# Matmul order inside a weight item: the products with the rounded weights first, those with the rest last

## The chip, the cores and the metric

One core of one Trainium2 chip runs the whole layer. The metric is the device time of one execution in microseconds (us); the figure given for a kernel is the median of its runs. PE is the matmul engine (TensorE), PEld its loads of the stationary operand, ACT is ScalarE, DVE is VectorE, POOL is GpSimd, and SP issues the DMAs that bring the weights.

## What is computed

One encoder layer on 256 tokens of width 2048 in float32: a norm, one input projection, eight heads of dilated attention beside eight heads of bidirectional retention, an output projection, and a SwiGLU feed-forward layer of width 5632, with residuals and a last norm. The part that the change touches is the second half:

```
h = h + mixed @ w_out
n2 = rmsnorm(h, norm_ffn_w)
h = h + (silu(n2 @ w_gate) * (n2 @ w_up)) @ w_down
return rmsnorm(h, norm_final_w)
```

## The kernel before

The matmuls run in a rounded form of float32 (float32r). To keep the precision, each operand is split in two: a rounded copy and a rest, which is the value less its rounded copy. A product a·w is then made of three matmuls: rounded with rounded, rounded with the weights' rest, and the activations' rest with the rounded weights. In the code `x[0]`, `x[1]` are the rounded and the rest part of the activations (the stationary operand, 128x128), `w[0]`, `w[1]` those of the weights (the moving operand, 128x512).

From the output projection on, the products are "by tokens": tokens are the rows of the result, and the weights stream past as tiles of 128 x 1024, one DMA of 512 KB each. A `Block` is a result of 256 tokens by 1024 columns (o0, o1 of the output projection, gu0 to gu10 of gate and up, d0_0 to d2_1 of down). It runs a list of items written in `ORDERS`. An item named "C" is a plain product: one weight tile serves four banks of PSUM (2, 3, 4 and 8: two token halves by two column halves), three matmuls each, twelve in all. An item with a number, 1 to 7, is one of the seven products of a Strassen scheme: one weight tile, one bank, six matmuls (two halves of the contraction, three each). "K" and "Z" are plain products of the last block, whose split weights are kept. "H" and "T" stand for the gating of the block before and for the transposes of its result (names `pt_h`, or `pt_n` for the normed input), "M" for the sums that join the seven products.

For each weight tile the work goes through three engines: SP loads the raw tile (`rawc`, `raw`, into a few fixed buffers), ACT copies it into the rounded half of a `ws` tile (L524), DVE subtracts to get the rest into the other half (L527), and PE multiplies (L581). There are five `ws` buffers and the split is issued three items ahead. Every instruction of ACT, DVE, POOL and PE in this part is chained to the one recorded before it on the same engine (`ch`), so each engine works in the order in which the code is written. DVE and ACT have other work in the same queue: DVE ends the blocks (`part`, `ht`), makes the sums of tiles, and the gating product (L758).

`Block.three` (L576 to L582) issues the three matmuls of one product; `classical` picks bank, activations and column half for one quarter of an item; `run` goes through the steps of an item and calls `done`, which lets DVE end a bank after its last matmul.

Of the kernel before, what the change touches and what calls it, by code (L numbers as in the profile page):

```python
# [88 lines left out]
def encoder_layer(ctx: ExitStack, tc: tile.TileContext, xT, x, gains, gain_f, decay, tab, w_qk, w_in, w_st, y):  # L89
# [8 lines left out]
    nc = tc.nc  # L98
# [31 lines left out]
    def wtile(name):  # L130
        return wsp.tile([P, 4, 2, CB], F32R, tag="ws", name=name)
# [134 lines left out]
    for c in range(KT // 2):  # L266
# [6 lines left out]
        src = w_qk[c].rearrange("p (k c) -> p k c", c=CB)  # L273
# [8 lines left out]
        ws = wtile(f"ws_first{c}")  # L282
        for k in range(0, 4, step):
            w, r = ws[:, k:k + step], half[:, k:k + step]
# [218 lines left out]
    def ch_ins(ins):  # L503

        if ins.engine in queue:
            tc.add_manual_dep(
                ins, queue[ins.engine].name,
                mybir.DependencyInfo(mybir.DependencyClass.NoSync, mybir.DependencyReason.DATA), reason="stream",
            )
        queue[ins.engine] = ins  # L510

    def ch(ins):
        ch_ins(ins.ins)
# [43 lines left out]
    class Block:  # L557
# [16 lines left out]
                self.banks[r] = ps1(f"p{r}_{self.name}")  # L574
            return self.banks[r]

        def three(self, r, x, w):

            for u, v in ((0, 0), (0, 1), (1, 0)):
                self.left[r] -= 1  # L580
                ch(nc.tensor.matmul(self.bank(r), x[u], w[v], start=r not in self.begun, stop=self.left[r] == 0))  # L581
                self.begun.add(r)  # L582

        def done(self, *rs):
            for r in rs:
# [50 lines left out]
            return ws  # L636

        def classical(self, ws, k, i, n):
            self.three((2, 3, 4, 8)[2 * i + n], self.quarter(self.a[k // 2], 2 * (k % 2) + i), ws[n])

        def run(self, what, m, ws):
            if what == "M":
                self.mid()
            elif what == "C":
                for i in range(2):
                    for n in range(2):
                        self.classical([[ws[:, q, v] for v in range(2)] for q in range(2)], m, i, n)
                self.done(2, 3, 4, 8)
            elif what == "K":
                self.kept.append((m, [[w[:, v] for v in range(2)] for w in ws]))  # L650
                for n in range(2):
                    self.classical(self.kept[-1][1], m, 0, n)
                self.done(2, 3)
            elif what == "Z":
                for n in range(2):
                    for k, w in self.kept:
                        self.classical(w, k, 1, n)
                    self.done((4, 8)[n])
            elif isinstance(what, int):
                src, q = {1: (self.a, 0), 2: (self.a, 2), 3: (self.sa, 3), 4: (self.a, 3),  # L660
                          5: (self.sa, 0), 6: (self.sa, 1), 7: (self.sa, 2)}[what]
                for u in range(2):
                    self.three(what, self.quarter(src[2 * m + u], q), [ws[:, u, v] for v in range(2)])
                if what in (2, 3, 4):
                    self.done(what)
            elif self.hooks.get(what):
                self.hooks[what].pop(0)()
# [149 lines left out]
    for i, (b, what, m) in enumerate(stream):  # L817
        done += i in work
        for k in work[:done + AHEAD]:
            if k >= i and k not in ready:  # L820
                c, w, n = stream[k]
# [78 lines left out]
```

## Time and profile before

| | us |
|---|---|
| median of 3 runs | 1170.35 (1169.21 to 1172.95) |
| the profiled execution | 1173.2 |
| its span | 1171.0 |
| PE busy | 1139.8 (97%) |
| DVE busy | 971.2 (83%) |
| ACT busy | 673.4 (58%) |
| stretch of the products by tokens (L581) | from 367 to 1161 of the span |

The profile is one execution. The page gives shares of the span; a busy PE in it is a modelled one, since the end of a matmul is not observed. More is learned from the starts: the timeline merges instructions of the same kind that follow each other into a row (start, length, count), and the difference of two rows' starts over the count is what one matmul costs there. A row ends in square brackets where the engine stood idle before it, with the instruction that ended the wait.

### The profile page before, as it was taken

The numbers are of one execution on the slowest core, as the hardware profiler recorded it, in microseconds if no ns is written. First come the engines' busy times: TensorE is split into PE (matmuls) and PEld (weight loads), VectorE is DVE, ScalarE is ACT, GpSimd is POOL, SyncE is SP. The second block draws the span as 40 slices with busy tenths as digits, with TensorE's granted clock in tenths as the row PEclk, the third lists the DMA queues.
The fourth block names the chain that finished last, engine by engine and source line by source line (L and its number), as shares of the span: only waits on it lengthen the run. The fifth ranks groups of instructions, "written<-read, shape, count | busy, mean of one in ns | idle before, by whom it ended". The sixth has DMA issues, their size and how long they took to land.

```text
span 1171.0 us, 15265 instructions
## 1 busy us (share of the span) xinstructions
PE 1139.8 (97%) x5546; PEld 953.4 (81%) x5546; DVE 971.2 (83%) x1053; ACT 673.4 (58%) x824; POOL 202.2 (17%) x198
## 2 busy tenths in 40 slices
PE   7999999999999999999999999999999999999996
PEld 5888888888887877878888878788888877888885
DVE  8887787576677787779998888899989878999985
ACT  6355555555655565556656555566666555666653
POOL 8432232112122110010000021000100202000011
PEclk9999999999999999999999999999999999999998
DMA  8664555555556877659888899988988899889785
GB/s 324 200 232 151 191 190 166 167 178 166 163 171 180 266 215 219 211 174 259 257 249 247 274 262 252 301 228 247 262 265 235 239 319 245 277 255 289 236 215 156
DMA packets 77115, 267.37 MB, mean 228 GB/s; under 512 B 8816, under 2 KB 8816, under 8 KB 77040
## 3 DMA queue, kind: packets, MB, share of 16 engines
q1 hardware_dynamic: 61920, 221.29, 54.3%
q0 software_dynamic: 14400, 44.05, 21.0%
q10 hardware_dynamic: 720, 1.07, 0.2%
q8 instruction: 43, 0.70, 0.2%
q14 instruction: 32, 0.26, 0.1%
HBM read 220.23 MB, written 2.10 MB: 190 GB/s over the span
## 4 chain that ended last, share of the span: by engine, by line
PE 74%; DVE 12%; DMA 7%; issue 4%; ACT 3%; POOL 0%; SPq 0%; DVEq 0%; POOLq 0%; ACTq 0%
PE p_gu L581 29%; PE p_d L581 13%; DVE ws_gu L527 3%; DMA rawc_d<-in_w_st 3%; PE ps_qr L157 3%; PE ps_va L164 3%; PE ps_gr L157 3%; PE ps_vr L164 3%; PE ps_kr L157 3%; PE p_o L581 2%; PE ps_ka L157 2%; DMA rawc_gu<-in_w_st 2%; PE ps_qa L157 2%; DMA rawc_o<-in_w_st 1%; DVE ws_o L527 1%
## 5 line engine op out<-in xcount | busy, mean ns | idle before, releaser
L581 PE MATMUL p_gu<-ws_gu,n 128*128 128x512 f32 x1482 | 355.9, 392 | 6.4 <-DVE ws_gu L527 4.8
L581 PEld LDWEIGHTS p_gu<-ws_gu,n 128*128 128x128 f32 x1482 | 278.4, 188 | 69.1 <-DVE ws_gu L527 8.9
L581 PE MATMUL p_d<-ws_d,h 128*128 128x512 f32 x708 | 168.9, 390 | 2.0 <-DVE ws_d L527 1.8
L527 DVE TENSOR_TENSOR ws_gu<-rawc_gu,ws_gu 128x1024 fp32r<-128x1024 f32 x113 | 137.7, 1220 | 29.2 <-ACT ws_gu L524 28.0
L581 PEld LDWEIGHTS p_d<-ws_d,h 128*128 128x128 f32 x708 | 132.6, 188 | 31.2 <-DVE ws_d L527 2.9
L524 ACT ACTIVATE ws_gu<-rawc_gu 128x1024 fp32r<-128x1024 f32 x113 | 118.8, 1056 | 53.5 <-PE p_gu L581 28.6
L581 PE MATMUL p_gu<-ws_gu,sa_n 128*128 128x512 f32 x504 | 128.5, 391 | 0.0
L581 PEld LDWEIGHTS p_gu<-ws_gu,sa_n 128*128 128x128 f32 x504 | 93.9, 188 | 19.2 <-DVE ws_gu L527 0.2
L527 DVE TENSOR_TENSOR ws_gu<-raw_gu,ws_gu 128x1024 fp32r<-128x1024 f32 x84 | 102.4, 1219 | 1.5 <-ACT ws_gu L524 0.5
L524 ACT ACTIVATE ws_gu<-raw_gu 128x1024 fp32r<-128x1024 f32 x84 | 88.5, 1054 | 22.3 <-PE p_gu L581 18.5
L527 DVE TENSOR_TENSOR ws_d<-rawc_d,ws_d 128x1024 fp32r<-128x1024 f32 x54 | 65.8, 1220 | 20.5 <-ACT ws_d L524 19.8
L524 ACT ACTIVATE ws_d<-rawc_d 128x1024 fp32r<-128x1024 f32 x54 | 57.2, 1059 | 37.8 <-DMA rawc_d<-in_w_st 19.8
L524 ACT ACTIVATE ws_gu<-rawt_gu 128x1024 fp32r<-128x1024 f32 x42 | 44.3, 1056 | 55.7 <-DVE rawt_gu L527 40.4
L537 POOL DMA_DIRECT2D raw_gu<-raw_gu x21 | 18.1, 862 | 290.9 <-DVE rawt_gu L527 209.9
L581 PE MATMUL p_d<-ws_d,sa_h 128*128 128x512 f32 x240 | 61.2, 390 | 0.0
L527 DVE TENSOR_TENSOR ws_gu<-rawt_gu,ws_gu 128x1024 fp32r<-128x1024 f32 x42 | 51.2, 1219 | 5.4 <-ACT ws_gu L524 5.4
L581 PEld LDWEIGHTS p_d<-ws_d,sa_h 128*128 128x128 f32 x240 | 44.8, 188 | 9.2
L524 ACT ACTIVATE ws_d<-raw_d 128x1024 fp32r<-128x1024 f32 x40 | 42.2, 1055 | 12.6 <-PE p_d L581 11.4
L527 DVE TENSOR_TENSOR ws_d<-raw_d,ws_d 128x1024 fp32r<-128x1024 f32 x40 | 48.7, 1219 | 0.7
L157 PE MATMUL ps_gr<-n,ws_gr 128*128 128x512 f32 x128 | 45.6, 399 | 0.0
L164 PE MATMUL ps_va<-ws_va,n 128*128 128x512 f32 x128 | 45.6, 399 | 0.0
L157 PE MATMUL ps_qr<-n,ws_qr 128*128 128x512 f32 x128 | 45.5, 399 | 0.0
(258 smaller groups left out, 2270.4 us busy)
## 6 DMA issues: line engine op xcount, KB each, us to landing
rawc_gu<-in_w_st SPq DMA_DIRECT2D x113, 512.0 KB, 5.2
raw_gu<-in_w_st SPq DMA_DIRECT2D x63, 512.0 KB, 5.3
rawc_d<-in_w_st SPq DMA_DIRECT2D x58, 512.0 KB, 5.1
raw_d<-in_w_st SPq DMA_DIRECT2D x30, 512.0 KB, 5.1
rawc_o<-in_w_st SPq DMA_DIRECT2D x23, 512.0 KB, 5.0
raw_gu<-raw_gu POOLq DMA_DIRECT2D x21, 512.0 KB, 7.4
raw_gu<-rawt_gu POOLq DMA_DIRECT2D x21, 512.0 KB, 5.6
raw_va<-in_w_in SPq DMA_DIRECT2D x16, 512.0 KB, 3.9
```

What stands on the lines that cost most here:

```text
L157: nc.tensor.matmul(ps[:, f, :], t[:, j, 0, f * P:(f + 1) * P], a, start=start, stop=False)
L164: nc.tensor.matmul(ps[:, f, :], a[:, 0, f * P:(f + 1) * P], t[:, j, :, :], start=first, stop=False)
L524: ch(nc.scalar.activation(out, src, func, **kw))
L527: ch(nc.vector.tensor_tensor(out, x, y, op=op))
L537: ch(nc.gpsimd.dma_start(out, other, accum_op=ALU.add))
L581: ch(nc.tensor.matmul(self.bank(r), x[u], w[v], start=r not in self.begun, stop=self.left[r] == 0))
```

## The change

Inside an item the matmuls are put in another order. Before, each bank (or, in a numbered item, each half of the contraction) had its three matmuls in a row: rounded with rounded, rounded with the weights' rest, the activations' rest with rounded. Now all matmuls that read the rounded weights come first, over all banks of the item, and those that read the weights' rest come last. A "C" item so has eight matmuls on the rounded half and then four on the rest; a numbered item four and two; a "K" item four and two. In the last "C" of a block (where `left[2] == 3`) and in "Z" the banks still follow each other, with the rest last inside each bank. The number of matmuls, weight loads and all other instructions is the same.

```
-        def three(self, r, x, w):
-
-            for u, v in ((0, 0), (0, 1), (1, 0)):
-                self.left[r] -= 1
-                ch(nc.tensor.matmul(self.bank(r), x[u], w[v], start=r not in self.begun, stop=self.left[r] == 0))
-                self.begun.add(r)
+        def products(self, *rxw):
+
+            for pairs in (((0, 0), (1, 0)), ((0, 1),)):
+                for r, x, w in rxw:
+                    for u, v in pairs:
+                        self.left[r] -= 1
+                        ch(nc.tensor.matmul(self.bank(r), x[u], w[v], start=r not in self.begun, stop=self.left[r] == 0))
+                        self.begun.add(r)
...
         def classical(self, ws, k, i, n):
-            self.three((2, 3, 4, 8)[2 * i + n], self.quarter(self.a[k // 2], 2 * (k % 2) + i), ws[n])
+            return (2, 3, 4, 8)[2 * i + n], self.quarter(self.a[k // 2], 2 * (k % 2) + i), ws[n]
...
             elif what == "C":
-                for i in range(2):
-                    for n in range(2):
-                        self.classical([[ws[:, q, v] for v in range(2)] for q in range(2)], m, i, n)
+                ws = [[ws[:, q, v] for v in range(2)] for q in range(2)]
+                each = [self.classical(ws, m, i, n) for i in range(2) for n in range(2)]
+                if self.left[2] == 3:
+                    for one in each:
+                        self.products(one)
+                else:
+                    self.products(*each)
                 self.done(2, 3, 4, 8)
             elif what == "K":
                 self.kept.append((m, [[w[:, v] for v in range(2)] for w in ws]))
-                for n in range(2):
-                    self.classical(self.kept[-1][1], m, 0, n)
+                self.products(*(self.classical(self.kept[-1][1], m, 0, n) for n in range(2)))
                 self.done(2, 3)
...
-                for u in range(2):
-                    self.three(what, self.quarter(src[2 * m + u], q), [ws[:, u, v] for v in range(2)])
+                self.products(*((what, self.quarter(src[2 * m + u], q), [ws[:, u, v] for v in range(2)]) for u in range(2)))
```

The first place is block d0_1, on PE: a numbered item (weights `ws_d_1_5939`, bank `p_d_1_5860`) and the "C" item behind it (weights `ws_d_1_5954`, four banks). A row is one form of matmul, "x3" a run of three; "waits" names the engine whose work has to be done first: Activation is ACT's rounded half, DVE the rest. Before:

```order
L581 MATMUL p_d_1_5860<-ws_d_1_5939,h_1_0_4902 128x512 [waits Activation_49]
L581 MATMUL p_d_1_5860<-ws_d_1_5939,h_1_0_4902 128x512 [waits DVE_49]
L581 MATMUL p_d_1_5860<-ws_d_1_5939,h_1_0_4902 128x512
L581 MATMUL p_d_1_5860<-ws_d_1_5939,h_1_1_4914 128x512 x3
L581 MATMUL p_d_1_5882<-ws_d_1_5954,h_2_1_5260 128x512 [waits Activation_49]
L581 MATMUL p_d_1_5882<-ws_d_1_5954,h_2_1_5260 128x512 [waits DVE_49]
L581 MATMUL p_d_1_5882<-ws_d_1_5954,h_2_1_5260 128x512
L581 MATMUL p_d_1_5895<-ws_d_1_5954,h_2_1_5260 128x512 x3
```

The same two items on PE now:

```order
L583 MATMUL p_d_1_5860<-ws_d_1_5939,h_1_0_4902 128x512 [waits Activation_49]
L583 MATMUL p_d_1_5860<-ws_d_1_5939,h_1_0_4902 128x512
L583 MATMUL p_d_1_5860<-ws_d_1_5939,h_1_1_4914 128x512 x2
L583 MATMUL p_d_1_5860<-ws_d_1_5939,h_1_0_4902 128x512 [waits DVE_49]
L583 MATMUL p_d_1_5860<-ws_d_1_5939,h_1_1_4914 128x512
L583 MATMUL p_d_1_5882<-ws_d_1_5954,h_2_1_5260 128x512 [waits Activation_49]
L583 MATMUL p_d_1_5882<-ws_d_1_5954,h_2_1_5260 128x512
L583 MATMUL p_d_1_5894<-ws_d_1_5954,h_2_1_5260 128x512 x2
L583 MATMUL p_d_1_5897<-ws_d_1_5954,h_2_1_5260 128x512 x2
L583 MATMUL p_d_1_5900<-ws_d_1_5954,h_2_1_5260 128x512 x2
L583 MATMUL p_d_1_5882<-ws_d_1_5954,h_2_1_5260 128x512 [waits DVE_49]
```

The wait for DVE has moved from the second matmul of an item to the fifth of a numbered item and to the ninth of a "C" item; the wait for ACT stands where it stood.

The second place is block gu1, on PE: its first "C" item and the transposes (`pt_h`) of the gated result of gu0 that follow it. Before:

```order
L581 MATMUL p_gu_4522<-ws_gu_4490,n_2_0_4207 128x512 [waits DVE_49]
L581 MATMUL p_gu_4522<-ws_gu_4490,n_2_0_4207 128x512
L581 MATMUL p_gu_4535<-ws_gu_4490,n_2_0_4207 128x512 x3
L581 MATMUL p_gu_4539<-ws_gu_4490,n_2_0_4207 128x512 x3
L581 MATMUL p_gu_4543<-ws_gu_4490,n_2_0_4207 128x512 x3
L693 MATMUL pt_h_00_4547<-ident,part_gu_4365 128x128 [waits DVE_49]
```

The same place on PE now:

```order
L583 MATMUL p_gu_4534<-ws_gu_4490,n_2_0_4207 128x512 x2
L583 MATMUL p_gu_4537<-ws_gu_4490,n_2_0_4207 128x512 [waits DVE_49]
L583 MATMUL p_gu_4537<-ws_gu_4490,n_2_0_4207 128x512
L583 MATMUL p_gu_4540<-ws_gu_4490,n_2_0_4207 128x512 [waits DVE_49]
L583 MATMUL p_gu_4540<-ws_gu_4490,n_2_0_4207 128x512
L583 MATMUL p_gu_4522<-ws_gu_4490,n_2_0_4207 128x512 [waits DVE_49]
L583 MATMUL p_gu_4534<-ws_gu_4490,n_2_0_4207 128x512
L583 MATMUL p_gu_4537<-ws_gu_4490,n_2_0_4207 128x512
L583 MATMUL p_gu_4540<-ws_gu_4490,n_2_0_4207 128x512
L697 MATMUL pt_h_00_4547<-ident,part_gu_4365 128x128 [waits DVE_49]
```

Here the third and fourth bank are opened at the fifth and seventh matmul instead of the seventh and tenth, with waits of their own for DVE's reading of their former contents; the transposes behind wait for DVE as before. On ACT, DVE, POOL and SP the order of the instructions is the same in both kernels.

## Rows read from the trace of the kernel before

**Rows 1.** Timeline of PE in block o1: start, length (us), engine, line, operation, count
```profile
428.79 1.52 PE L581 MATMUL p_o<-ws_o,sa_ma 128*128 128x512 f32 x6
430.15 2.88 PE L581 MATMUL p_o<-ws_o,ma 128*128 128x512 f32 x12
432.87 2.88 PE L581 MATMUL p_o<-ws_o,mr 128*128 128x512 f32 x12
```

**Rows 2.** Waits of PE: who waited for whom, us in total, times, longest
```profile
PE p_gu L581 <- DVE ws_gu L527: 4.8, 9, 0.9
```

**Rows 3.** Timeline of PE in blocks d0_1 and gu4
```profile
693.11 1.86 PE L581 MATMUL p_d<-ws_d,h 128*128 128x512 f32 x7
695.72 4.15 PE L581 MATMUL p_d<-ws_d,h 128*128 128x512 f32 x17 [0.76 <-DVE ws_d L527]
...
737.17 0.50 PE L581 MATMUL p_gu<-ws_gu,n 128*128 128x512 f32 x1 [0.58 <-ACT ws_gu L524]
738.43 4.19 PE L581 MATMUL p_gu<-ws_gu,n 128*128 128x512 f32 x17 [0.76 <-DVE ws_gu L527]
```

**Rows 4.** Timeline of PE in block gu5
```profile
778.73 1.75 PE L581 MATMUL p_gu<-ws_gu,n 128*128 128x512 f32 x7
780.65 4.16 PE L581 MATMUL p_gu<-ws_gu,n 128*128 128x512 f32 x17 [0.17 <-DVE ws_gu L527]
784.64 1.52 PE L581 MATMUL p_gu<-ws_gu,sa_n 128*128 128x512 f32 x6
```

**Rows 5.** Timeline of PE late in block gu1
```profile
525.91 1.75 PE L581 MATMUL p_gu<-ws_gu,n 128*128 128x512 f32 x7
528.10 4.19 PE L581 MATMUL p_gu<-ws_gu,n 128*128 128x512 f32 x17 [0.44 <-DVE ws_gu L527]
```

**Rows 6.** Timeline of PE at the first "C" of the last block, d2_1
```profile
1132.32 1.75 PE L581 MATMUL p_d<-ws_d,h 128*128 128x512 f32 x7
1134.41 2.79 PE L581 MATMUL p_d<-ws_d,h 128*128 128x512 f32 x11 [0.34 <-DVE ws_d L527]
```

**Rows 7.** Timeline of PE at the first "C" of block o1
```profile
415.06 0.49 PE L581 MATMUL p_o<-ws_o,ma 128*128 128x512 f32 x1 [0.43 <-ACT ws_o L524]
416.31 2.79 PE L581 MATMUL p_o<-ws_o,ma 128*128 128x512 f32 x11 [0.77 <-DVE ws_o L527]
```

**Rows 8.** Timeline of PE early in block gu0
```profile
459.67 0.40 PE L581 MATMUL p_gu<-ws_gu,n 128*128 128x512 f32 x1
460.81 1.45 PE L581 MATMUL p_gu<-ws_gu,n 128*128 128x512 f32 x5 [0.74 <-DVE ws_gu L527]
463.11 0.51 PE L581 MATMUL p_gu<-ws_gu,n 128*128 128x512 f32 x1 [0.86 <-ACT ws_gu L524]
464.37 4.39 PE L581 MATMUL p_gu<-ws_gu,n 128*128 128x512 f32 x11 [0.76 <-DVE ws_gu L527]
468.60 1.03 PE L693 MATMUL pt_n<-ident,ht 128*128 128x128 f32 x8
```

**Rows 9.** Timeline of PE at the first "C" of block gu1 and the transposes behind it
```profile
508.49 1.75 PE L581 MATMUL p_gu<-ws_gu,n 128*128 128x512 f32 x7
511.11 2.81 PE L581 MATMUL p_gu<-ws_gu,n 128*128 128x512 f32 x11 [0.87 <-DVE ws_gu L527]
514.86 0.33 PE L693 MATMUL pt_h<-ident,part_gu 128*128 128x128 f32 x1 [0.94 <-DVE part_gu L758]
```

**Rows 10.** Timeline of ACT, DVE at the same place: the gating of gu0
```profile
507.45 2.48 DVE L527 TENSOR_TENSOR part_gu<-p_gu,part_gu 128x512 f32<-128x512 f32 x4
...
513.29 1.33 ACT L524 ACTIVATE part_gu<-part_gu,r 128x512 f32<-128x512 f32 x2 [6.20 <-POOL r L731]
...
514.05 1.41 DVE L758 SCALAR_TENSOR_TENSOR part_gu<-part_gu,r,part_gu 128x512 f32<-128x512 f32 x2 [1.59 <-ACT part_gu L524]
```

**Rows 11.** Busy time of each engine by stretch, then PE's granted clock, DMA share, GB/s
```profile
699.71:735.07 35.36, 35.36 (x157) 29.28 (x156) 29.89 (x30) 17.81 (x18) 6.99 (x8) 1.00 0.93 267
464.69:468.10 3.41, 3.41 (x9) 2.67 (x8) 2.41 (x2) 2.23 (x6) 0.00 (x0) 0.50 0.79 250
```

More of the change, by code (lines that the diff above doesn't have):

```diff
@@ L656, in run @@
                     for k, w in self.kept:
-                        self.classical(w, k, 1, n)
+                        self.products(self.classical(w, k, 1, n))
                     self.done((4, 8)[n])
```

## The prediction

> **What bounds the kernel now.** I read the timeline of PE first, for what a matmul costs when nothing holds it; then PE's waits; then, for each wait on a weights' rest, the rows around it and what the engine that ends it was doing; last, one stretch without waits.
>
> The starts give the pace: six matmuls into one bank take 430.15 - 428.79 = 1.36 us, twelve over four banks 432.87 - 430.15 = 2.72 us, so 0.227 us each in both [rows 1]. A row that needs more than its count times 0.227 until the next row starts has lost the difference. PE is the bound nearly everywhere: from 699.71 to 735.07 it is busy for all of the 35.36 us, with DVE at 29.89 [rows 11]. What it loses, it loses in short waits, and the largest group is PE waiting for `ws_gu`'s rest from DVE, nine times [rows 2]. The pattern is the same each time: the first matmul of an item runs, since ACT's rounded half is there, and the second, the first to read the rest, waits. I found fourteen such places: those nine, four in o1, d0_1, d1_1 and d2_1, and one in gu6 that is too short to be marked as a wait.
>
> **The change part by part.** Nothing is removed or added: same matmuls, same loads of stationary operands, same order on ACT, DVE, POOL and SP. What moves is the point at which an item needs the rest: from 1 x 0.227 us after its start to 8 x 0.227 = 1.81 us in a "C" item and to 4 x 0.227 = 0.91 us in a numbered one.
>
> How late is the rest? At the worst "C" places the second matmul starts 1.25 to 1.26 us after the first [rows 7, 8], the pace alone would make it 0.23; so the rest is there 1.25 us after the start, 0.56 us before the new order asks for it. The whole wait goes in a "C" item. In the one numbered item of the fourteen the second matmul starts 460.81 - 459.67 = 1.14 us after the first [rows 8], 0.23 us later than the new 0.91; most goes.
>
> After a wait PE also loses something at the restart: from 780.65 to 784.64 seventeen matmuls take 3.99 us instead of 3.86, 0.13 us [rows 4]. Where a wait for ACT stays in front, I leave that cost in.
>
> Now place by place, each against the profiled execution.
>
> - Two "C" items whose weights arrive just in time: 695.72 - 693.11 = 2.61 us for seven matmuls worth 1.59, so 1.02, and 0.13 for the restart: 1.15 [rows 3]. The pattern stands twice (d0_1 and gu8): 2.30.
> - Two more where ACT is late too: 738.43 - 737.17 - 0.23 = 1.03 [rows 3], twice (gu4, d1_1): 2.06. ACT's part stays.
> - Blocks gu2, gu5, gu6 and gu9, in which DVE is behind with the sums of the tiles: 780.65 - 778.73 - 1.59 = 0.33, with the restart 0.46 [rows 4], four times: 1.84.
> - gu1, late: 528.10 - 525.91 - 1.59 = 0.60, with the restart 0.73 [rows 5].
> - d2_1: 1134.41 - 1132.32 - 1.59 = 0.50, with the restart 0.63 [rows 6].
> - o1: 416.31 - 415.06 - 0.23 = 1.02 [rows 7].
> - gu0, "C": 464.37 - 463.11 - 0.23 = 1.03 [rows 8].
>
> Two places I count at nothing. The numbered item at 459.67 would win most of its 0.91 us, but the next item waits for ACT anyway (0.86 idle at 463.11, [rows 8]); PE comes there earlier and waits longer. And the "C" at 509.85 would win 1.03, but behind it stand transposes that already wait 0.94 us for DVE's gating [rows 9], and that chain is not PE's: DVE ends gu0 from 507.45, ACT's gating starts at 513.29 when POOL lets it, DVE's at 514.05 when ACT does [rows 10]. PE arrives about a microsecond earlier at 514.86 and waits as much more.
>
> Sum: 2.30 + 2.06 + 1.84 + 0.73 + 0.63 + 1.02 + 1.03 = 9.6 us.
>
> Does a microsecond won at one place survive to the end? It does where the stretch behind is PE's own, as 699.71 to 735.07 is: there weights wait for PE to free a `ws` buffer, so everything that feeds PE moves with it. What is late next is DVE, by the same amount as before, but with 1.6 us (seven matmuls) more room in a "C".
>
> Edits that I cost at nothing, with their cover. The third and fourth bank of a "C" are opened at its fifth and seventh matmul, up to 0.7 us earlier than before, and must be read out by then. At gu1 these readings end at 507.45 + 2.48 = 509.93 [rows 10], the fifth matmul would come at 509.85 + 0.91. If that cover were gone, the first "C" of each of the 19 blocks would lose up to 0.7 us, 13 us in all; I take nothing, as the row says. The activations' rest is needed one matmul earlier; nobody waits for it now. The banks' ends: in the last "C" of a block and in numbered items the last matmul of a bank stands where it stood, so DVE gets each block as early as before. In the last "K" bank 2 is finished two matmuls later, 0.45 us, with "Z" (24 matmuls, 5.4 us) behind it. A `ws` buffer is freed by the item's last matmul in both orders.
>
> One cost has no row of its own: 138 of the 156 "C" items now change bank with every one of their last four matmuls. The nearest row is the "C" item that changes every three: no cost in 2.72 us [rows 1], so I take zero; the other end is a restart of 0.13 us per item [rows 4].
>
> The Trainium skill speaks against such an order: its page "TensorE: Matmul & The Clock Gate", section "A second HAM failure mode: psum-queue depth-cycling", tells of a kernel that cycled through PSUM banks, idled briefly between groups and so lost throughput to a swinging clock. In this trace items over four banks keep the pace of items in one. By the row the sum stays 9.6; by the rule it would turn into a loss, the fourth rival below.
>
> The clock has one more term. Behind the three waits of gu0 PE ran from 464.69 to 468.10 at half its clock, granted 0.50, 1.2 GHz [rows 11], and the eleven matmuls from 464.37 took 468.60 - 464.37 = 4.23 us instead of 2.49 [rows 8]. Less the restart that is 1.6 us. In the new order PE idles there once, not three times, so the clock may stay up; I leave this out of the sum and put it into the low end.
>
> **The rivals.**
>
> 1. *More is won.* The clock stays up in gu0 (1.6), and the two places counted at nothing keep part of their 1.9 us. Up to 13 us off: 1157.3. Against it: both places have a wait of another chain right behind.
> 2. *Part is absorbed.* If late weights are set by the DMAs' own rate (share 0.93 in the stretch, [rows 11]) and not by PE's releases, the four places of the first two bullets give their 4.4 us back as waits for ACT, and so may o1 (1.0), which has one in front. Then 4.2 us remain: 1166.1. For it: at 415.06, 463.11 and 737.17 PE already waits for ACT. Against it: PE's full busy time between two such places.
> 3. *DVE is the bound* and the waits only move: no change, 1170.4. Against it: in the stretch of rows 11 DVE is 5.5 us short of busy.
> 4. *Slower: the banks.* Changing bank with each matmul makes PE pause once in each of the 138 items, at a restart's price: 138 x 0.13 = 18 us, less 9.6: 1178.7. It decides from 0.07 us per item. No row shows a pause at a change of bank.
>
> That the change doesn't do what it says is excluded by the order of the program.
>
> **How the numbers follow.** The profiled execution took 1173.2 us, 2.85 above the median of 1170.35. The sum is made on the profiled one and gives 1163.6 there; off the median it gives 1170.35 - 9.6 = 1160.8. Chances: forecast (8 to 11 us off) 0.55; rival 1 0.12; rival 2 0.18; rival 3 0.09; rival 4 0.06. The range goes from rival 1's 1157.3 to rival 2's 1166.1, rounded outwards by what the runs of before scatter: 1157.0 to 1166.5; outside lie rivals 3 and 4, 0.15, and a little of the others. About 0.3%, 3.5 us, is what a measurement of this kernel can tell from no change: faster 0.85, same 0.09, slower 0.06.
>
> **What would show it.** PE's waits for the rest in "C" items are gone from its list; those for ACT at 415, 463 and 737 are still there, and the one for DVE's L758 before the transposes of gu1 has grown from 0.94 to about 2 us idle. Twelve matmuls of a "C" still take 2.72 us; if they take 2.8 or more, rival 4 is at work. If the waits for ACT grow by what the waits for DVE lost, rival 2 is. The forecast is wrong if DVE's waits turn up again one item later, or if the half clock comes up at more places than one.

## The result and the profile after

The changed kernel takes 1163.51 us (median of 6 runs, 1162.26 to 1165.43), the kernel before, measured beside it, 1171.88 (6 runs, 1169.21 to 1174.09). The ratio is 0.993, with a 95% interval from 0.9912 to 0.9948: 8.2 us faster, between 6.1 and 10.3. Built and run a second time beside other kernels, it came out at 0.9944 (0.9927 to 0.9961), 6.6 us. Both fit 7 to 8 us.

The profiled execution took 1162.26 us, its span 1160.2. From the page of the changed kernel: busy times, the chain that ended last by engine, and the group of the gate and up matmuls (busy, mean ns of one | idle ahead of it).

```profile
PE 1131.2 (98%) x5546; PEld 949.8 (82%) x5546; DVE 969.2 (84%) x1053; ACT 672.4 (58%) x824; POOL 201.9 (17%) x198
...
PE 83%; DVE 7%; DMA 4%; issue 3%; ACT 2%; POOL 0%; SPq 0%; DVEq 0%; POOLq 0%; ACTq 0%
...
L583 PE MATMUL p_gu<-ws_gu,n 128*128 128x512 f32 x1482 | 351.6, 390 | 2.3 <-ACT ws_gu L524 2.3
```

The span is 10.8 us shorter. DVE, ACT and POOL are busy as long as before, within 2 us, and a matmul of this group has a mean of 390 ns, 392 before; what idle time the group has left is charged to ACT and no longer to DVE. On the chain PE's share is 83%. The same two lines of the kernel before:

```profile
PE 74%; DVE 12%; DMA 7%; issue 4%; ACT 3%; POOL 0%; SPq 0%; DVEq 0%; POOLq 0%; ACTq 0%
...
L581 PE MATMUL p_gu<-ws_gu,n 128*128 128x512 f32 x1482 | 355.9, 392 | 6.4 <-DVE ws_gu L527 4.8
```

PE's waits show where it came from. Of the kernel before, the lines for the rest (L527) beside that of [rows 2], and the one for the gating (us in total, times, longest):

```profile
PE p_d L581 <- DVE ws_d L527: 1.8, 3, 0.8
PE p_gu L581 <- ACT ws_gu L524: 1.4, 2, 0.9
PE pt_h L693 <- DVE part_gu L758: 1.3, 2, 0.9
PE p_o L581 <- DVE ws_o L527: 0.8, 1, 0.8
```

Of the changed kernel, the lines of the products by tokens:

```profile
PE pt_h L697 <- DVE part_gu L762: 2.9, 2, 2.5
PE p_gu L583 <- ACT ws_gu L524: 2.3, 2, 1.3
...
PE pt_n L697 <- DVE n L716: 0.7, 1, 0.7
```

In this part no wait for a rest is left: 4.8 + 1.8 + 0.8 = 7.4 us before, none after. Three others have grown or are new: those ahead of gu1's transposes from 1.3 to 2.9, for ACT's rounded half from 1.4 to 2.3, and 0.7 ahead of the second transposes of gu0. Together they took 3.2 us back. The list counts idle time alone; from start to start a place cost more than its wait (1.08 us at d0_1, where the wait was 0.76), so the account below, made from starts, comes out above 7.4 - 3.2.

The same on PE's timeline of the changed kernel (start, length, count, idle ahead of it), at the places of [rows 3], [rows 8] and [rows 9]:

```profile
457.76 1.52 PE L583 MATMUL p_gu<-ws_gu,n 128*128 128x512 f32 x6
460.31 3.02 PE L583 MATMUL p_gu<-ws_gu,n 128*128 128x512 f32 x12 [1.04 <-ACT ws_gu L524]
...
511.25 0.33 PE L697 MATMUL pt_h<-ident,part_gu 128*128 128x128 f32 x1 [2.54 <-DVE part_gu L762]
...
688.22 5.69 PE L583 MATMUL p_d<-ws_d,h 128*128 128x512 f32 x24
693.74 1.52 PE L583 MATMUL p_d<-ws_d,sa_h 128*128 128x512 f32 x6
...
731.88 4.42 PE L583 MATMUL p_gu<-ws_gu,n 128*128 128x512 f32 x18 [1.26 <-ACT ws_gu L524]
```

At 457.76 (gu0) the numbered item runs through, and the wait for ACT behind it is 1.04 us, 0.86 in [rows 8]. At 688.22 (d0_1) the numbered item, the "C" and the numbered item behind it run through: 24 matmuls in 693.74 - 688.22 = 5.52 us, 0.230 each. Before, the same 24, the 7 and 17 of [rows 3], took from 693.11 to 699.71, 6.60 us. At 731.88 (gu4) the wait for the rest is gone, but that for ACT ahead of the item is 1.26 us instead of the 0.58 of [rows 3]. At 511.25 PE stands 2.54 us where it stood 0.94 in [rows 9].

The first matmul of each block in both timelines gives the account by stretches, beside the prediction's terms:

| stretch | predicted us won | won in the profiles |
|---|---|---|
| o1 | 1.02 | 0.93 |
| gu0 | 1.03 | 2.48 |
| gu1 | 0.73 | 0.02 |
| gu2, gu5, gu6, gu9 | 1.84 | 0.49 + 0.49 + 0.44 + 0.51 = 1.93 |
| d0_1, gu8 | 2.30 | 1.08 + 1.06 = 2.14 |
| gu4, d1_1 | 2.06 | 0.35 + 1.41 = 1.76 |
| d2_1 | 0.63 | 0.55 |
| all other blocks | 0 | 0.07 |
| sum | 9.61 | 9.88 |

A further 0.94 us lies ahead of o0, in a part of the program that did not change, where the granted clock was at half at other moments. And of gu0's 2.48, 1.6 are the half clock of [rows 11], which is not there in this execution of the changed kernel. So 8.3 us are the waits' own. In the second profile of the changed kernel the same stretches give 8.05 us, with a half clock of its own, in gu1. Over whole executions the granted clock doesn't tell the two kernels apart: 0.994 in the mean of the 33 runs of the kernel before beside the experiments, single ones 0.991 to 0.998, and 0.994 in the mean of twelve of the changed one, 0.990 to 0.998.

### The profile page after: what moved, and what is told of

Read it like the earlier page. It is cut to its first block, busy times and chain, and to the rows that moved or that the text cites. A ratio compares the mean times of both kernels' runs of the same rounds, so it can differ in the third digit from the quotient of the medians.

```text
span 1160.2 us, 15265 instructions
## 1 busy us (share of the span) xinstructions
PE 1131.2 (98%) x5546; PEld 949.8 (82%) x5546; DVE 969.2 (84%) x1053; ACT 672.4 (58%) x824; POOL 201.9 (17%) x198
## 3 DMA queue, kind: packets, MB, share of 16 engines
q10 hardware_dynamic: 720, 1.07, 0.3%
## 4 chain that ended last, share of the span: by engine, by line
PE 83%; DVE 7%; DMA 4%; issue 3%; ACT 2%; POOL 0%; SPq 0%; DVEq 0%; POOLq 0%; ACTq 0%
PE p_gu L583 35%; PE p_d L583 17%; PE ps_qr L157 3%; PE ps_gr L157 3%; PE ps_va L164 3%; PE ps_vr L164 3%; PE ps_kr L157 3%; PE p_o L583 2%; PE ps_ka L157 2%; PE ps_qa L157 2%; DMA rawc_o<-in_w_st 1%; PE ps_kr L158 1%; PE ps_vr L165 1%; PE ps_va L165 1%; PE ps_gr L158 1%
## 5 line engine op out<-in xcount | busy, mean ns | idle before, releaser
L583 PE MATMUL p_gu<-ws_gu,n 128*128 128x512 f32 x1482 | 351.6, 390 | 2.3 <-ACT ws_gu L524 2.3
L527 DVE TENSOR_TENSOR ws_gu<-rawc_gu,ws_gu 128x1024 fp32r<-128x1024 f32 x113 | 137.2, 1219 | 27.7 <-ACT ws_gu L524 26.6
L527 DVE TENSOR_TENSOR ws_gu<-raw_gu,ws_gu 128x1024 fp32r<-128x1024 f32 x84 | 102.3, 1217 | 1.3 <-ACT ws_gu L524 0.5
L527 DVE TENSOR_TENSOR ws_d<-rawc_d,ws_d 128x1024 fp32r<-128x1024 f32 x54 | 65.6, 1219 | 20.3 <-ACT ws_d L524 19.8
L527 DVE TENSOR_TENSOR ws_gu<-rawt_gu,ws_gu 128x1024 fp32r<-128x1024 f32 x42 | 51.2, 1219 | 5.5 <-ACT ws_gu L524 5.4
L527 DVE TENSOR_TENSOR ws_d<-raw_d,ws_d 128x1024 fp32r<-128x1024 f32 x40 | 48.7, 1218 | 0.5
L524 ACT ACTIVATE ws_d<-raw_d 128x1024 fp32r<-128x1024 f32 x40 | 42.1, 1054 | 10.8 <-PE p_d L583 9.2
```

The lines of the kernel that those rows point to most:

```text
L524: ch(nc.scalar.activation(out, src, func, **kw))
L527: ch(nc.vector.tensor_tensor(out, x, y, op=op))
```

## The experiments

**Theory:** a "C" item wins the time by which its rest is late, since it asks for it at the ninth matmul and not at the second; nothing else in the new order has a price. **Rivals:** the order itself makes PE faster or slower (two matmuls in a row on the same moving operand, changes of bank), or the numbered items carry a good part.

### The "C" items alone, and all but the "C" items

First kernel, numbered items, "K", "Z" and the last "C" of a block in the old order (`three`, as it was):

```
             elif what == "C":
...
                     for one in each:
-                        self.products(one)
+                        self.three(*one)
                 else:
                     self.products(*each)
...
-                self.products(*((what, self.quarter(src[2 * m + u], q), [ws[:, u, v] for v in range(2)]) for u in range(2)))
+                for u in range(2):
+                    self.three(what, self.quarter(src[2 * m + u], q), [ws[:, u, v] for v in range(2)])
```

> The new order stands in the "C" items alone; numbered items, "K" and "Z" have the old one. Theory (the gain is the wait for the rest, moved from the second matmul of a "C" to its ninth): all but one of the fourteen places are "C" items, and what the numbered one in gu0 won was taken back by the wait for ACT behind it. So 7.5 to 9 us faster than before, as much as the whole change. Rival (the gain comes from some other effect of the order, which every item has): the 95 or so numbered items keep the old order, so a part of the gain goes, 2 us or more.

Second kernel, the other way round, every "C" in the old order:

```
-                if self.left[2] == 3:
-                    for one in each:
-                        self.products(one)
-                else:
-                    self.products(*each)
+                for one in each:
+                    self.three(*one)
```

> The other half: the new order in numbered items, "K" and "Z", the old one in every "C". Theory: at most the 0.9 us of the one numbered place in gu0, so 0 to 1.5 us faster than before, and PE's nine waits for ws_gu's rest are all but one still there. Rival (another effect of the order): 2 us or more.

Measured: the "C" items alone 1164.71 us, ratio 0.9947 (0.9934 to 0.9959), 6.2 us faster; the rest of the change alone 1172.09 against 1171.56, ratio 1.0011 (1.0 to 1.0022), no gain and perhaps a small loss. So the gain is the "C" items'. (The numbered items are 238, not the 95 or so of the expectation; the argument doesn't change.) The 6.2 is below what was expected, 7.5 to 9, though its interval (4.8 to 7.7) overlaps with that of the whole change. The traces say what the numbered half does. PE's timeline at the start of gu0, "C" items alone:

```profile
455.74 0.39 PE L589 MATMUL p_gu<-ws_gu,sa_n 128*128 128x512 f32 x1
456.76 1.43 PE L589 MATMUL p_gu<-ws_gu,sa_n 128*128 128x512 f32 x5 [0.64 <-DVE ws_gu L527]
458.03 0.40 PE L589 MATMUL p_gu<-ws_gu,n 128*128 128x512 f32 x1
459.16 1.43 PE L589 MATMUL p_gu<-ws_gu,n 128*128 128x512 f32 x5 [0.73 <-DVE ws_gu L527]
461.46 3.06 PE L583 MATMUL p_gu<-ws_gu,n 128*128 128x512 f32 x12 [0.88 <-ACT ws_gu L524]
```

Since o1 now ends earlier, two numbered items wait, not one, and the "C" behind them begins at 461.46 instead of 460.31. In the whole change neither waits; in its second profile the "C" begins at 460.89. So the numbered half is worth 0.6 to 1.2 us there, but only once the "C" half has brought PE forward.

The same piece of gu1 without the "C" half (PE's timeline):

```profile
508.54 0.39 PE L589 MATMUL p_gu<-ws_gu,n 128*128 128x512 f32 x1
511.37 2.83 PE L589 MATMUL p_gu<-ws_gu,n 128*128 128x512 f32 x11 [2.44 <-DVE ws_gu L527]
```

In this execution the half clock of gu0 was absent and the "C" of gu1 began 1.3 us earlier, at 508.54; before, by [rows 9], it was 508.49 + 6 x 0.227 = 509.85. The second matmul came at 511.37 all the same, where it was 511.11 before. What was won ahead of that point is lost in it: DVE makes this rest behind its ending of gu0, and that began at 507.71, no earlier than the 507.45 of [rows 10]. This one profile can't be set against that of the kernel before for the total: it has a half clock in gu4, from 739.04 to 742.45, and lost 1.8 us there.

### The point at which the rest is asked for

Two kernels with the changed order in numbered items, and the "C" items bank by bank, or by pairs of banks:

```
-                if self.left[2] == 3:
-                    for one in each:
-                        self.products(one)
-                else:
-                    self.products(*each)
+                for one in each:
+                    self.products(one)
```

> Every "C" goes bank by bank with the rest last inside each bank; so its first rest is asked for by the third matmul, 0.45 us after its start, and each weights' half is still followed by the same two stationary loads as in the whole change. Numbered items as in the whole change. Theory: each of the 13 places wins one matmul, 0.227 us: 13 x 0.227 = 3.0 us faster at most, with what is taken back later 1.5 to 3. Rival (two matmuls on the same moving operand in a row are what is faster): 8 us, as in the whole change.

```
                 else:
-                    self.products(*each)
+                    self.products(*each[:2])
+                    self.products(*each[2:])
```

> A "C" is done in two pairs of banks: four matmuls on the rounded weights, two on the rest, and again; the first rest is asked for by the fifth matmul, 0.91 us after the start. Theory: the six places that wait about 1.02 us win 0.68 each, the other seven all of theirs: 6 x 0.68 + 4 x 0.46 + 0.73 + 0.63 = 7.3 us at most, with what is taken back later 5 to 7.3. Rival (the last matmuls of a "C" without a bank change, or fewer of them, are what counts): nothing between 3 and 8 us in particular, nearer to one of its neighbours.

Measured: third matmul 1167.00 us, ratio 0.9968 (0.9955 to 0.998), 3.7 us faster; fifth 1164.72, ratio 0.9948 (0.9935 to 0.9962), 6.1 us. PE's waits, first of the third matmul, then of the fifth:

```profile
PE p_gu L583 <- DVE ws_gu L527: 2.7, 7, 0.5
...
PE pt_h L694 <- DVE part_gu L759: 1.5, 2, 1.2
...
PE p_d L583 <- DVE ws_d L527: 1.0, 2, 0.5
PE p_o L583 <- DVE ws_o L527: 0.5, 1, 0.5
```

```profile
PE pt_h L698 <- DVE part_gu L763: 2.0, 2, 1.6
...
PE p_gu L583 <- DVE ws_gu L527: 0.8, 2, 0.6
```

The rest asked for at the second, third, fifth and ninth matmul leaves PE waiting 7.4, 4.2, 0.8 and 0 us for it, in one profile each, and the wait ahead of gu1's transposes goes the other way: 1.3, 1.5, 2.0, 2.9. The times follow the first and are held back by the second: 0, 3.7, 6.1, and 8.2 or 6.6. The third-matmul kernel puts the same two products on the rounded half in a row as the whole change and gets about half of the gain (3.7 us of 8.2 or 6.6), so the pairs don't account for it, and the waits do. It won a little more than the 1.5 to 3 expected, within its interval (2.3 to 5.3). Fifth and ninth can't be told apart by their times, only by their waits.

### The price of a change of bank

```
-        def products(self, *rxw):
+        def products(self, *rxw, by=(((0, 0), (1, 0)), ((0, 1),))):
...
-            for pairs in (((0, 0), (1, 0)), ((0, 1),)):
+            for pairs in by:
...
                 else:
-                    self.products(*each)
+                    self.products(*each, by=(((0, 0),), ((1, 0),), ((0, 1),)))
```

> The changed kernel, but the eight matmuls on the rounded weights of a "C" go over the four banks twice (all four with the activations' rounded part, then all four with their rest), so each of the twelve matmuls changes bank; in the changed kernel seven of the twelve do. The rest is still asked for by the ninth. 138 items, 4 more changes of bank each. Theory (a change of bank costs nothing): the time of the changed kernel within 1 us, twelve matmuls in 2.72 us. Rival (each change costs something, paid already in the changed kernel and hidden in its gain): 138 x 4 = 552 more changes at c each; at 0.13 us per item as in the prediction's fourth rival, shared by four changes, 18 us slower than the changed kernel; the smallest that can be told is about 1.5 us, 3 ns a change.

> The changed kernel once more, beside the three below. All theories: 8.4 us faster than before, as measured, give or take 1.5.

Measured: 1165.28 us, ratio 0.9947 (0.9931 to 0.9962), beside 1164.23, 0.9944 (0.9927 to 0.9961), for the changed kernel in the same comparison. PE's timeline in d0_1 with the bank changed at each matmul, and a long stretch by windows (stretch, its length, busy us of PE, PEld, DVE, ACT, POOL with counts, granted clock, DMA share, GB/s):

```profile
703.87 2.88 PE L583 MATMUL p_d<-ws_d,h 128*128 128x512 f32 x12
706.59 1.52 PE L583 MATMUL p_d<-ws_d,sa_h 128*128 128x512 f32 x6
```

```profile
700.00:734.00 34.00, 33.95 (x150) 27.79 (x148) 27.77 (x28) 15.92 (x17) 6.99 (x8) 1.00 0.94 266
```

The twelve matmuls of a "C", with a change each, take 706.59 - 703.87 = 2.72 us, as before; the clock is 1.00. The 1.05 us between the medians is within what these runs scatter; were it all the 552 changes', it would be 2 ns each. The pause of the prediction's fourth rival, 18 us, is not there. In this stretch PE is idle for 0.05 of the 34.00 us. The loss by cycling through banks that the Trainium skill tells of (page "TensorE: Matmul & The Clock Gate", section "A second HAM failure mode: psum-queue depth-cycling") is tied there to PE idling briefly between groups. That idling is not found here, and neither is the loss. Elsewhere PE does wait for a rest in this profile, 0.2 us in gu0 and 0.82 at the ninth matmul of gu1's first "C": asking at the ninth is not late enough there each time.

### What was taken back: gu1, the opening, the start of gu0

A second "C" ahead of the transposes of gu1:

```
 MAIN = "1a 5a H 2a C T 3a C 6a C 7a 1b C 4a 5b C 2b 6b C 7b M C C 3b 4b"
...
+    "gu_second": "1a 5a H 2a C C T 3a C 6a 7a 1b C 4a 5b C 2b 6b C 7b M C C 3b 4b",
     "main": MAIN,
...
-        out.append(["gu_first" if fb == 0 else "main" for fb in range(lo, hi)])
+        out.append([{0: "gu_first", 1: "gu_second"}.get(fb, "main") for fb in range(lo, hi)])
```

> The changed kernel with another order of items in block gu1 alone: a second "C" stands ahead of the transposes ("2a C C T 3a C 6a 7a" instead of "2a C T 3a C 6a C 7a"), so these come 2.72 us later on PE; nothing is added. Theory (in gu1 the chain of DVE and ACT that ends gu0 and gates it sets the time, and what PE had won before is lost in the wait of 2.54 + 0.33 us in front of the transposes): that wait is gone, 2 to 3 us faster than the changed kernel, 10 to 11.5 faster than before. Rival (PE's wait there is covered, or the second "C" waits for its own weights, whose split stands in DVE's queue behind the gating): no gain, and a wait for ws_gu of the same size ahead of the transposes or behind them.

Measured: 1162.41 us, ratio 0.9923 (0.9908 to 0.9938), 9.0 us faster than before and 1.8 better than the changed kernel beside it, somewhat under the 2 to 3 expected. Its PE timeline:

```profile
509.02 3.93 PE L584 MATMUL p_gu<-ws_gu,n 128*128 128x512 f32 x16 [0.65 <-DVE ws_gu L528]
512.78 0.32 PE L698 MATMUL pt_h<-ident,part_gu 128*128 128x128 f32 x1
513.43 0.98 PE L698 MATMUL pt_h<-ident,part_gu 128*128 128x128 f32 x7 [0.33 <-DVE part_gu L763]
```

The 2.54 us ahead of the transposes are gone, and the second "C" runs through: the row of 16 is the last four matmuls of the first "C" and the twelve of the second. The wait of 0.65 for a rest is that of the first "C", ahead of the edit; the kernel above, with the old order here, has one of 0.82 at the same matmul, and the two last kernels, with the new order, have none. What is new behind the transposes is a wait of 0.28 us later in gu1, far from the size that the rival asks for. From the first matmul of gu1 to that of gu2 it needs 44.79 us, the changed kernel 45.37 in one profile and 46.76 in the other; why these two differ is told below.

The same edit in the opening, where a tile's matmuls on the rounded half now all come ahead of those on the rest:

```
-        for i in range(2):
-            for f in range(2):
-                mm_feature(firsts[i], (ws, 2 * i + f), n1[2 * c + f], c + f == 0, 2 * c + f == KT - 1, i == 0)
+        for half in range(2):
+            for i in range(2):
+                for f in range(2):
+                    mm_half(half, firsts[i], (ws, 2 * i + f), n1[2 * c + f], c + f == 0, 2 * c + f == KT - 1, i == 0)
```

(`mm_feature` issues a tile's matmuls on the two halves in turn; `mm_half` issues those on one half alone.)

> The changed kernel, with the same edit in the opening too: of each tile of ws_first the eight matmuls on the rounded half first, then the eight on the rest, instead of in turn; the rest is asked for by the ninth matmul, some 1.8 us after the start, and not by the second. There PE waits 7.8 us for the rest, seven times. Theory (the tiles come at a pace that DVE, ACT and the DMAs set, so PE only waits elsewhere, and the stage ends earlier by no more than one tile's wait of 0 to 2 us): 0 to 2 us faster than the changed kernel. Rival (the waits add up as they do in the products by tokens): 5 to 7.8 us faster.

Measured: 1163.09 us, ratio 0.9931 (0.9915 to 0.9947), 1.1 us under the changed kernel beside it, which these runs can't tell from nothing. PE's waits in it:

```profile
PE ps_first L166 <- DVE n L254: 2.9, 7, 0.6
...
PE ps_first L168 <- DVE ws_first L296: 2.4, 5, 0.6
```

The 7.6 to 7.8 us of waiting for the rest in the two profiles of the changed kernel became 2.4, and 2.9 for something else that DVE delivers (the normed input, `n`): the waits moved. The first matmul behind the opening comes at 37.72 us instead of 39.18 and 39.45; at o0, 330 us later, 0.4 to 0.5 of that is left. The rival, that all waits add up, falls. That the tiles come at a pace that the other engines set fits, but was not measured by itself.

All three places together, and in gu0 the second pair of transposes later:

```
-    "gu_first": "1a 5a 2a C T C C T C 3a 6a C 7a C 4a M C C C C C C",
+    "gu_first": "1a 5a 2a C T C C 3a T C 6a C 7a C 4a M C C C C C C",
```

> The changed kernel with three further edits together: the order of gu1 and that of the opening from the two experiments before, and in block gu0 the second pair of transposes one numbered item later ("C T C C 3a T C" instead of "C T C C T C 3a"), since PE waits 0.3 to 0.7 us for DVE in front of it. Theory (the three lie at different places, and what is won in one stage is kept where the next is PE's own): 1.8 from gu1, about 1 from the opening, up to 0.7 from gu0, so 2.5 to 3.5 us faster than the changed kernel and 10 to 11 faster than before. Rival (the gains are taken back by the wait for ACT at the start of gu0, which grows when PE comes earlier, so that nothing won before 460 us counts): 1.8 to 2.5 us faster than the changed kernel.

and with ACT's squares of `ht` three items later:

```
     def end_out(block, i, n, bank):
...
+        if block.q and (i, n) == (0, 0):
+            later.extend([lambda: None] * 3)
         later.append(lambda: square(sums_h, block.q + n, i))
```

> As the one before, and ACT's four squares of ht behind the end of o1 are issued three items later. In ACT's queue the first of them waits 3.3 us for DVE in front of the split of the first "C" of gu0, for which PE then waits 1.0 to 1.6 us. Theory (it is this square that makes the split late): the wait for ACT at 460 us is gone; DVE ends that tile's rest at about 461.5, 0.6 us after the ninth matmul would then ask for it, so 0.4 to 1 us faster than without this edit. Rival (the tile itself lands late there): no difference, and ACT waits for the DMA at that place.

Measured: 1161.14 us, ratio 0.9905 (0.9888 to 0.9921), and 1159.82 us, ratio 0.9895 (0.988 to 0.991): 11.1 and 12.3 us faster than before. The first fits the 10 to 11 expected. Its rival isn't ruled out by its time, as the changed kernel did not run beside it, and PE's wait for ACT at the start of gu0 is 1.57 us in it. The second is the fastest kernel of the study. ACT's timeline at the start of gu0 in the changed kernel:

```profile
458.59 0.63 ACT L524 ACTIVATE q<-ht 128x512 f32<-128x512 f32 x1 [3.34 <-DVE ht L527]
...
459.22 1.04 ACT L524 ACTIVATE ws_gu<-rawc_gu 128x1024 fp32r<-128x1024 f32 x1
```

In the fastest kernel, ACT's and then PE's:

```profile
455.11 3.13 ACT L536 ACTIVATE ws_gu<-rawc_gu 128x1024 fp32r<-128x1024 f32 x3
458.55 0.63 ACT L536 ACTIVATE q<-ht 128x512 f32<-128x512 f32 x1 [0.30 <-DVE ht L539]
```

```profile
457.97 2.57 PE L595 MATMUL p_gu<-ws_gu,n 128*128 128x512 f32 x10 [0.20 <-DVE ws_gu L539]
461.50 1.19 PE L595 MATMUL p_gu<-ws_gu,n 128*128 128x512 f32 x4 [0.96 <-DVE ws_gu L539]
```

The split was late because the square stood ahead of it: three splits now run at 455.11, and PE waits for no rounded half there. The rest takes its place as the last arrival, as expected, but at the ninth matmul: DVE ends it at 461.5, and PE waits 0.96 us, where 0.6 was expected. The step from 1161.14 to 1159.82 lies within the intervals, and the profile of the kernel without this edit has a half clock at that place (below); that the wait for ACT is gone is seen, its price by time is not settled. Nor is it settled how much of what these two kernels won is the clock's: it is 0.996 to 0.998 in the runs of the one and 0.997 to 0.998 in those of the other.

## Why the prediction held, and where it was off

The forecast was 1160.8 us with a range from 1157.0 to 1166.5; 1163.51 lies inside, 2.7 above the forecast. By its steps:

- **The mechanism** is shown: waits for the rest 7.4, 4.2, 0.8, 0 us as the point of asking moves back, and the time with them. "C" alone gives the gain, the rest of the change alone none.
- **The places** where PE's own work lies behind came out nearly to the tenth: 1.93 for 1.84 in the four blocks with sums, 2.14 for 2.30 in d0_1 and gu8, 0.55 for 0.63 in d2_1, 0.93 for 1.02 in o1. In the four blocks 0.48 each fits the 0.46 with the restart, not the 0.33 without it. One profile against one is no surer than a few tenths: in the second profile o1 gives 1.36 and d0_1 and gu8 1.81.
- **gu1's 0.73** was mis-sized: that wait was indeed won, 0.78 us between the first matmuls of neighbouring items, but the stretch as a whole gave 0.02. The prediction saw that the wait for the gating would grow there. It took for granted that only what PE won inside gu1 would go into it. A part of what was won ahead went into it too: gu1 began 4.36 us earlier (505.77 and 501.41), its transposes only 3.61 (514.86 and 511.25). PE's wait there became 2.54 us, not the about 2 foretold. In the second profile 0.55 us were lost in the same way, and 1.6 to a half clock.
- **gu4's 1.03** was mis-sized: 0.35 came out, because the wait for ACT ahead of the item grew by 0.68. That is rival 2 at one of the places that it named; at d1_1, named as well, 1.41 came out, more than was counted, since ACT is not late there either. In the second profile the two gave 0.63 and 1.07.
- **The numbered item at 459.67**, counted at nothing, won 0.9, and the second transposes of gu0, a place that the prediction didn't look at, gave 0.87 back by a wait of 0.69 for DVE. The value was right by luck in this profile, as the two cancel, and the reason holds only in part: the next wait for ACT grew by just 0.2. In the second profile the reason holds: that wait is 1.57 us, and the numbered item won nothing.
- **The clock term** of 1.6 us was rightly kept out of the sum: the half clock went from gu0 in one profile and stood in gu1 in the other.
- **The base:** the sum was taken off a median of three runs, 1170.35. The kernel before, run again beside the experiments 15, 11 and 7 times, has medians of 1171.56, 1170.85 and 1171.94, and 1171.88 beside the result. Off the last the forecast would have been 1162.3. So about half of the 2.7 us is the base, and the other half is of the size of what gu1 and gu4 took back.
- **The rivals** of the prediction: 3 (DVE is the bound) is out, as PE's waits for it are gone with DVE's busy time unchanged; 4 (the banks) is out by the kernel that changes bank each time; 1 would have been 13 us, more than the interval's 10.3; 2 is right for about 0.7 of its 5.4 us.

## To carry to other kernels

Where an operand is prepared in two steps, let the consumer first do all the work that needs only the first step, across all its accumulators: the slack grows from one instruction to most of an item, and costs nothing if changing the accumulator is free, which a short experiment tells. Sum such gains place by place and ask at each one which wait comes next: behind it, PE's own work keeps the gain, while a wait for another engine's chain (here the gating ahead of gu1's transposes) takes back a part of it, 0.75 of 4.36 us here, or all of it, 1.3 us in the kernel without the "C" half. The same edit in the opening moved the waits and hardly the end of the kernel.

## What the runs showed of the hardware

In these traces the granted clock falls to half behind waits of PE, but not each time, and the size of the wait alone doesn't decide it. Of the six profiles in which PE stood 2.3 us or more in gu1 behind the first "C" or in it, four have a stretch at half clock (0.50, 1.2 GHz) of 3.4 us at that place, two have none, with the same program in one pair. The changed kernel, profiled the second time (PE's timeline, then the window):

```profile
511.28 0.33 PE L697 MATMUL pt_h<-ident,part_gu 128*128 128x128 f32 x1 [2.56 <-DVE part_gu L762]
511.94 0.98 PE L697 MATMUL pt_h<-ident,part_gu 128*128 128x128 f32 x7 [0.33 <-DVE part_gu L762]
512.68 2.46 PE L583 MATMUL p_gu<-ws_gu,sa_n 128*128 128x512 f32 x6
514.93 3.71 PE L583 MATMUL p_gu<-ws_gu,n 128*128 128x512 f32 x12
```

```profile
513.21:516.62 3.41, 3.41 (x9) 2.63 (x8) 2.88 (x5) 3.35 (x6) 0.00 (x0) 0.50 0.44 154
```

And the same window of the first profile, with a wait of 2.54 us ahead of it:

```profile
513.21:516.62 3.41, 3.41 (x16) 2.81 (x15) 2.87 (x5) 3.35 (x6) 0.00 (x0) 1.00 0.51 154
```

Nine matmuls in one, sixteen in the other: some 1.6 us of work (gu1 as a whole is 1.39 us longer), about a fifth of the whole gain, come and go between executions of one program. In the kernels without such a wait in gu1 (the rest at the third or fifth matmul, the second "C" ahead of the transposes, and the two last) no stretch at half clock lies there. Three more lie elsewhere between the opening and the end of the products: in gu0 of the kernel before, behind waits of 0.74, 0.86 and 0.76 us ([rows 8] and [rows 11]); in gu4 of the kernel without the "C" half, behind 0.81 and 0.77; and in gu0 of the kernel with the three places together, behind 1.57, a wait (1.56 or 1.57) that stands at that place in seven other profiles with no half clock behind it:

```profile
460.68:464.09 3.41, 3.41 (x9) 2.63 (x9) 2.74 (x3) 3.41 (x9) 0.00 (x0) 0.50 0.84 197
```

So the wait that the change lengthens at gu1 can cost more than its microseconds show; that this is why the kernel with the second "C" won 1.8 us, where the profiles account for 0.6 without a half clock and 2.0 with one, fits, but was not measured by itself.
